# Low halves of the projection weights: two ScalarE copies and an adding DMA in place of a GpSimd subtraction

## The chip, the cores and the metric

One Trainium2 chip, one of its cores. The time is that of one execution on the device in microseconds (us), from runs of the whole kernel; a profile of one execution gives the span from the first to the last instruction and what each engine did in it. Engines are named as in the profile: PE (TensorE matmul), PEld (its weight loads), DVE (VectorE), ACT (ScalarE), POOL (GpSimd), SP (SyncE, which issues most DMAs here).

## What is computed

A hybrid decoder block on 1040 tokens (16 meta tokens and 1024 of the sequence) of width 1024, all in float32:

```python
u = rms_norm(h, norm_mix_g[l])
proj = u @ w_in[l]
q, k, v, r, a_lr, c_in, g_gla, g_conf = jnp.split(proj, pts, axis=-1)
log_a = log_sigmoid(a_lr @ w_alpha_up[l] + b_alpha[l]) / GATE_TAU
o = gla_chunked(qh, kh, vh, ah)            # gated linear attention, 4 heads
br_gla = (rms_norm(o) * silu(r)) @ w_gla_o[l]
c = causal_dwconv(c1 * sigmoid(c2), conf_dw_w[l], conf_dw_b[l])   # 31 taps
br_conf = silu(layer_norm(c)) @ w_conf_o[l]
h = h + (sigmoid(g_gla) * br_gla + sigmoid(g_conf) * br_conf) @ w_out[l]
u = rms_norm(h, norm_ffn_g[l])
a, bv = jnp.split(u @ w_up[l], 2, axis=-1)
h = h + (silu(causal_dwconv(a, ffn_dw_w[l], ffn_dw_b[l])) * bv) @ w_down[l]
```

The change concerns the first product, `u @ w_in`, which with the work laid between its blocks takes the first 875 us.

## The kernel before

**Products in three parts.** Every large product is taken in a rounded type (float32r) and repaired: a number is split into a high half `hi`, the number rounded, and a low half `lo`, the number minus `hi`. `mm3` (lines 169 to 180) issues three matmuls for each piece of 128 input channels: weight `hi` by activation `hi` (L178), weight `hi` by activation `lo` (L179), weight `lo` by activation `hi` (L180). The split of a weight is made on the chip: `load_raw` (L153) has SP load 128 output columns of a weight (512 KB) into one of three buffers `wr`; in `split_w` ACT copies it with rounding into `wh` (L161) and another engine subtracts, `wl = wr - wh` (L162). `wh` and `wl` have three buffers each. Activations are split in the same way by `split` (L218, L219) into `uh` and `ul`.

**The stage.** The projection is 57 blocks: one for the 16 decay channels (`wh_a`, which carries both halves in one tile and has no `wl`), then q, k, v and the two convolution halves c2, c1 of each of four heads, r, and two gates. A block is 72 matmuls: 8 pieces of the input channels, three parts, three chunks of tokens. `next_w` keeps one weight ahead of the block that runs. The weights of blocks 1 to 50 of the list have the subtraction on POOL, those after them on DVE:

```python
wq.append(load_alpha(src) if src is w_alpha else load_w(src, PO if wpos[0] < 51 else V, rate["ahead"]))
```

**What runs between.** Into the blocks the attention steps of a head (`gla`) and the 31-tap convolutions (`conv`) are laid by a rate per evacuated chunk (`tick`). A conv step is one DVE instruction over 128 x 1026 (L361), 240 of them. `gla` alternates between engines: decays on ACT and DVE, exponent tiles E of seven levels, whose left half DVE makes and whose right half POOL makes (L460, L463 and L461, L464), with an exponential on ACT between them (L462), small matmuls on PE, copies of their results into Pt (L485, L502), then the state st from chunk to chunk (L515). kmT (L435) is the transposed key of the meta tokens, which ACT copies out for PE (L437).

**What sets the order.** A scheduler lays the instructions of each engine into one fixed queue ahead of time; each queue runs in order and waits where an operand or a buffer is not ready. Weight loads and splits are given a priority some thousands of instructions ahead of their place (`high_priority`).

Of the kernel before, what the change touches and what calls it, by code (L numbers as in the profile page):

```python
# [11 lines left out]
F32R = mybir.dt.float32r  # L12
U8 = mybir.dt.uint8
AF = mybir.ActivationFunctionType
ALU = mybir.AluOpType

P = 128
# [47 lines left out]
def build(ctx, tc, xT, w_mix, w_o3, w_up, w_dn, w_au, pvec, masks, outT):  # L65
    nc = tc.nc
    V, S, PO, PE = nc.vector, nc.scalar, nc.gpsimd, nc.tensor
# [4 lines left out]
    wspl = ctx.enter_context(tc.tile_pool(name="wspl", bufs=3))  # L72
    sm = ctx.enter_context(tc.tile_pool(name="sm", bufs=2))
    uid = [0]
# [13 lines left out]
    def slot(dt=F32, nm="s"):  # L88
        uid[0] += 1
        return slots.tile([P, SLOT], dt, tag="slot", name=f"{nm}_{uid[0]}")  # L90
# [55 lines left out]
    def pin(ins):  # L146
        if rate["pinned"]:
            tc.keep_in_program_order(ins)

    def load_raw(src):  # L150
        uid[0] += 1
        raw = wraw.tile([P, 1024], F32, tag="raw", name=f"wr_{uid[0]}")[:, : src.shape[-1]]
        nc.sync.dma_start(raw, src)  # L153
        return raw

    def split_w(raw, eng=None):
        uid[0] += 1
        n = raw.shape[-1]
        hi = wspl.tile([P, 1024], F32R, tag="hi", name=f"wh_{uid[0]}")[:, :n]
        lo = wspl.tile([P, 1024], F32R, tag="lo", name=f"wl_{uid[0]}")[:, :n]  # L160
        pin(S.activation(hi, raw, AF.Copy))  # L161
        (eng or V).tensor_tensor(lo, raw, hi.bitcast(F32), op=ALU.subtract)  # L162
        return hi, lo

    def load_w(src, eng=None, ahead=4000):
        with tc.high_priority(offset=ahead):
            return split_w(load_raw(src), eng)

    def mm3(out, whi, wlo, pairs, cols, first=True, last=True):
        n = len(pairs)  # L170
# [126 lines left out]
    def prefetch(n):  # L297
        while wpos[0] < len(seq) and len(wq) < n:
            src = seq[wpos[0]]
            wq.append(load_alpha(src) if src is w_alpha else load_w(src, PO if wpos[0] < 51 else V, rate["ahead"]))  # L300
            wpos[0] += 1
# [511 lines left out]
    def unit_tail(f, a, b, y):  # L813
# [7 lines left out]
        return y  # L821

    heads = [unit_head(load_w(w_up[0]))]
    for _ in due:
        pass
    heads += [unit_head(load_w(w_up[f])) for f in range(1, HEADS_UP)]
    w = slice(0, 2 * HT)
    ws = [unit_weights(0)]
# [62 lines left out]
    for j in range(FT // 2):  # L891
        if j == FT // 2 - 1:
            hi, lo = slot(F32R, "oph"), slot(F32R, "opl")
# [116 lines left out]
```

## Time and profile before

| what | value |
|---|---|
| runs, median (three) | 1897.48 us (1896.18 to 1898.14) |
| profiled execution, span from first to last instruction | 1894.4 us |
| mean granted TensorE clock | 0.980 |
| PE busy | 1786.0 us, 94% |
| DVE busy | 1228.9 us, 65% |
| ACT busy | 669.3 us, 35% |
| POOL busy | 570.3 us, 30% |
| DMA | 174.72 MB, mean 92 GB/s |

The profiled execution is given by its span alone; what lies around it, launch and end, is not in the profile, and the median of the runs is 3.1 us longer than the span. The share of busy time is a mean over stages: the projection ends at about 875 us, the three output products at 1152, the upward product of the feed-forward part at 1620, and the rest is the downward product. Which engine sets the pace of a stretch is read from the views by stretch, and what it waits for from the view of waits; the timeline shows single instructions. A row of the timeline has start, duration, engine, line, operation, and in brackets the idle time of that engine before it with what ended it.

### The profile page before, as it was taken

The page shows a single profiled execution, that of the slowest core. Times are in us where ns is not written, and L with a number is a line of the kernel's source. Part 1 is how long each engine was busy: PE and PEld are TensorE (multiplying, and loading weights), DVE is VectorE, ACT ScalarE, POOL GpSimd, SP SyncE. Part 2 cuts the span into 40 slices and gives each one's busy share as a digit, 9 for nine tenths or more (in the row PEclk, how much of TensorE's full clock was granted, in tenths as well). Part 3 has the DMA queues.
Part 4 walks back from the last instruction along what each step waited for, and adds up shares of the span by engine and source line. Part 5 has one row for each costly group of instructions (what it writes and reads, how often), then busy time and mean ns, then how long its engine had stood idle before and what let it go on. Part 6 is the DMA issues. An engine that isn't in the chain of part 4 may idle for free.

```text
span 1894.4 us, 28989 instructions
## 1 busy us (share of the span) xinstructions
PE 1786.0 (94%) x12210; PEld 1697.8 (90%) x12210; DVE 1228.9 (65%) x1462; ACT 669.3 (35%) x1008; POOL 570.3 (30%) x333
## 2 busy tenths in 40 slices
PE   5998999999899989999999998899999999899997
PEld 3997989898898989999999998899999999677886
DVE  7258969969899494354255467886676676643533
ACT  5314325324333752476132343222222222432321
POOL 3323624624542452210000144533333334200000
PEclk9998999999999999999999999899999999999999
DMA  4111111111110322436122532222212223644541
GB/s 172 45 45 45 35 45 68 34 45 56 45 45 23 101 68 78 156 114 232 51 92 82 195 121 97 68 79 90 79 67 90 79 69 112 248 123 133 165 133 64
DMA packets 56242, 174.72 MB, mean 92 GB/s; under 512 B 6064, under 2 KB 13360, under 8 KB 56112
## 3 DMA queue, kind: packets, MB, share of 16 engines
q1 hardware_dynamic: 51168, 159.03, 25.2%
q0 software_dynamic: 3168, 11.54, 1.7%
q10 hardware_dynamic: 1776, 2.30, 0.4%
q8 instruction: 96, 1.57, 0.4%
q14 instruction: 34, 0.28, 0.0%
HBM read 136.10 MB, written 36.74 MB: 91 GB/s over the span
## 4 chain that ended last, share of the span: by engine, by line
PE 55%; DVE 4%; issue 1%; ACT 0%; POOL 0%; DVEq 0%; ACTq 0%
PE prod L178 12%; PE prod L180 12%; PE prod L179 12%; PE mm L178 6%; PE mm L179 6%; PE mm L180 6%; DVE opl L219 1%; DVE un L713 1%; DVE wl L162 1%; PE g L934 1%; DVE un L831 0%; POOL opl L219 0%; DVE t L228 0%; ACT wh L161 0%; DVE fy L814 0%
## 5 line engine op out<-in xcount | busy, mean ns | idle before, releaser
L178 PE MATMUL mm<-uh,wh 128*128 128x342 f32 (+4 forms) x1344 | 447.8, 333 | 0.0
L179 PE MATMUL mm<-ul,wh 128*128 128x342 f32 (+4 forms) x1344 | 437.9, 326 | 0.0
L180 PE MATMUL mm<-uh,wl 128*128 128x342 f32 (+4 forms) x1344 | 436.2, 325 | 0.0
L361 DVE SCALAR_TENSOR_TENSOR y<-c,pv,y 128x1026 f32<-128x1026 f32 x240 | 390.0, 1625 | 5.2
L161 ACT ACTIVATE wh<-wr 128x1024 fp32r<-128x1024 f32 (+2 forms) x202 | 200.4, 994 | 488.6 <-PE mm L179 182.7
L179 PE MATMUL prod<-opl,wh 128*128 128x258 f32 x1232 | 349.6, 284 | 12.1 <-DVE opl L219 11.6
L178 PE MATMUL prod<-oph,wh 128*128 128x258 f32 x1232 | 349.9, 284 | 4.6 <-DVE t L796 3.5
L180 PE MATMUL prod<-oph,wl 128*128 128x258 f32 x1232 | 350.7, 285 | 0.0
L162 POOL TENSOR_TENSOR wl<-wr,wh 128x1024 fp32r<-128x1024 f32 x68 | 184.8, 2718 | 313.3 <-ACT wh L161 313.3
L162 DVE TENSOR_TENSOR wl<-wr,wh 128x1024 fp32r<-128x1024 f32 (+2 forms) x134 | 156.8, 1172 | 176.0 <-ACT wh L161 170.0
L178 PEld LDWEIGHTS mm<-uh,wh 128*128 128x128 f32 x1344 | 258.1, 192 | 3.9 <-issue 2.1
L179 PEld LDWEIGHTS mm<-ul,wh 128*128 128x128 f32 x1344 | 258.0, 192 | 3.2 <-issue 2.1
L180 PEld LDWEIGHTS mm<-uh,wl 128*128 128x128 f32 x1344 | 258.3, 192 | 0.9 <-issue 0.6
L179 PEld LDWEIGHTS prod<-opl,wh 128*128 128x128 f32 x1232 | 235.0, 191 | 13.2 <-DVE opl L219 12.5
L178 PEld LDWEIGHTS prod<-oph,wh 128*128 128x128 f32 x1232 | 235.1, 191 | 5.6 <-issue 3.2
L180 PEld LDWEIGHTS prod<-oph,wl 128*128 128x128 f32 x1232 | 234.8, 191 | 0.0
L180 PE MATMUL mm<-oph,wl 128*128 128x512 f32 (+1 forms) x374 | 143.8, 385 | 3.2 <-DVE wl L162 3.2
L178 PE MATMUL mm<-oph,wh 128*128 128x512 f32 (+1 forms) x374 | 143.8, 384 | 2.1 <-ACT wh L161 1.3
L179 PE MATMUL mm<-opl,wh 128*128 128x512 f32 (+1 forms) x374 | 144.8, 387 | 0.6 <-DVE opl L219 0.6
L178 PE MATMUL prod<-sh,wh 128*128 128x342 f32 (+2 forms) x448 | 133.6, 298 | 0.5 <-ACT gate L620 0.5
L180 PE MATMUL prod<-sh,wl 128*128 128x342 f32 (+2 forms) x448 | 133.3, 298 | 0.0
L179 PE MATMUL prod<-sl,wh 128*128 128x342 f32 (+2 forms) x448 | 133.3, 297 | 0.0
(238 smaller groups left out, 2763.6 us busy)
## 6 DMA issues: line engine op xcount, KB each, us to landing
wr<-in_w_mix SPq DMA_DIRECT2D x56, 512.0 KB, 3.3
wr<-in_w_up SPq DMA_DIRECT2D x48, 512.0 KB, 3.3
wr<-in_w_o SPq DMA_DIRECT2D x32, 512.0 KB, 3.5
wr<-in_w_dn SPq DMA_DIRECT2D x32, 512.0 KB, 3.6
act_d<-fy SPq DMA_DIRECT2D x21, 512.0 KB, 2.6
ar<-act_d POOLq DMA_DIRECT2D x21, 512.0 KB, 7.1
wr<-in_w_dn SPq DMA_DIRECT2D x16, 384.0 KB, 3.2
y_d<-y SPq DMA_DIRECT2D x8, 513.0 KB, 4.3
```

Of the source, the lines that this page charges most:

```text
L161: pin(S.activation(hi, raw, AF.Copy))
L162: (eng or V).tensor_tensor(lo, raw, hi.bitcast(F32), op=ALU.subtract)
L178: PE.matmul(out, whi[:, wk], hi[:, c0:c1], start=first and k == 0, stop=False)
L179: PE.matmul(out, whi[:, wk], lo[:, c0:c1], start=False, stop=False)
L180: PE.matmul(out, wlo[:, wk], hi[:, c0:c1], start=False, stop=last and k == n - 1)
L219: (eng or V).tensor_tensor(lo, src, hi.bitcast(F32), op=ALU.subtract)
L361: V.scalar_tensor_tensor(y[:, :LQ], c[:, j : j + LQ], pcol("dw_w", i * CONV_K + j), y[:, :LQ], op0=ALU.mult, op1=ALU.add)
L713: V.scalar_tensor_tensor(pair_cols(un[hf][j], 0, width)[:, e], pair_cols(hh[j], 0, width)[:, e], pcol("ffn_g", 2 * j + e), rs[:, :width], ...
L934: PE.matmul(stats[c], ones, sq, start=n == 1, stop=n == KT - 1)
```

## The change

For the 50 weights whose subtraction was on POOL, ACT writes two tiles from the raw weight: the rounded weight with its sign turned into `wl`, and the rounded weight into `wh`. Then POOL issues a DMA that reads the raw weight from memory once more and adds it into `wl`, so that `wl` is raw minus rounded. The other weights (the decay block, the last six of the projection, and all of the later stages) are split as before.

```diff
     def load_w(src, eng=None, ahead=4000):
         with tc.high_priority(offset=ahead):
-            return split_w(load_raw(src), eng)
+            raw = load_raw(src)
+            if eng is not PO:
+                return split_w(raw, eng)
+            uid[0] += 1
+            hi = wspl.tile([P, 1024], F32R, tag="hi", name=f"wh_{uid[0]}")
+            lo = wspl.tile([P, 1024], F32R, tag="lo", name=f"wl_{uid[0]}")
+            pin(S.activation(lo, raw, AF.Copy, scale=-1.0))
+            pin(S.activation(hi, raw, AF.Copy))
+            nc.gpsimd.dma_start(lo, src, accum_op=ALU.add)
+            return hi, lo
```

Nine lines are added, so that what stood at line 173 or below stands nine lines further down: L178 is now L187, L218 is L227. The two copies are L173 and L174, the adding DMA is L175.

The queues change in three places. First ACT at the start of the kernel, from the last steps of the first norm on. Before (`wh` and `wl` are weights, `uh` the activation's high half, x and t512 the input and its squares):

```order
L225 ACTIVATE t512_38_174<-t512_38_174 128x256
L161 ACTIVATE wh_67_363<-wr_66_361 128x1024
L161 ACTIVATE wh_69_369<-wr_68_367 128x1024
L218 ACTIVATE uh_11_106<-x_3_98 128x256
L218 ACTIVATE uh_13_108<-x_4_99 128x256
L218 ACTIVATE uh_15_110<-x_5_100 128x256
L267 ACTIVATE t512_40_206<-x_3_98 128x392
```

The same place of ACT's queue now:

```order
L234 ACTIVATE t512_38_174<-t512_38_174 128x256
L173 ACTIVATE wl_67_364<-wr_66_361 128x1024
L174 ACTIVATE wh_67_363<-wr_66_361 128x1024
L173 ACTIVATE wl_69_371<-wr_68_368 128x1024
L174 ACTIVATE wh_69_370<-wr_68_368 128x1024
L173 ACTIVATE wl_71_378<-wr_70_375 128x1024
L227 ACTIVATE uh_11_106<-x_3_98 128x256
L276 ACTIVATE t512_40_206<-x_3_98 128x392
```

Five weight copies stand ahead of the first activation copy where two stood; the fifth is the low half of the third weight, whose high half comes much later. Second, POOL's queue at that place, with the three adds ahead of the activation's low halves (before, two subtractions stood there):

```order
L175 DMA wl_67_364<-in_w_mix 128x1024
L175 DMA wl_69_371<-in_w_mix 128x1024
L175 DMA wl_71_378<-in_w_mix 128x1024
L228 TENSOR_TENSOR ul_14_109<-x_4_99,uh_13_108 128x256
L228 TENSOR_TENSOR ul_18_113<-x_6_101,uh_17_112 128x256
```

Later in POOL's queue each add stands, but for a few, where the subtraction stood. Third, PE where the first head's kmT is used, in the first v block of the second head (g are the attention's small products, mm the block). Before:

```order
L180 MATMUL mm_164_1415<-uh_15_110,wl_144_1275 128x348
L437 MATMUL g_157_1394<-vmeta_137_1219,kmT_156_1392 128x256
L448 MATMUL g_161_1401<-ident_81,kd_149_1341 128x128 x4
L178 MATMUL mm_164_1415<-uh_17_112,wh_144_1274 128x348
L179 MATMUL mm_164_1415<-ul_18_113,wh_144_1274 128x348
```

Now:

```order
L189 MATMUL mm_164_1427<-uh_15_110,wl_144_1285 128x348
L187 MATMUL mm_164_1427<-uh_17_112,wh_144_1284 128x348
L188 MATMUL mm_164_1427<-ul_18_113,wh_144_1284 128x348
L189 MATMUL mm_164_1427<-uh_17_112,wl_144_1285 128x348
L187 MATMUL mm_164_1427<-uh_19_114,wh_144_1284 128x348
L188 MATMUL mm_164_1427<-ul_20_115,wh_144_1284 128x348
L189 MATMUL mm_164_1427<-uh_19_114,wl_144_1285 128x348
L446 MATMUL g_157_1405<-vmeta_137_1229,kmT_156_1403 128x256
L457 MATMUL g_161_1412<-ident_81,kd_149_1352 128x128 x4
```

The two small products stand six matmuls of the block later; the same holds for the second and third heads.

## Rows read from the trace of the kernel before

**Rows 1.** Stretches: us, busy PE, PEld, DVE, ACT, POOL (instructions), clock, DMA share, GB/s.
```profile
0.00:16.00 16.00, 4.68 (x9) 2.15 (x9) 8.83 (x26) 7.04 (x11) 5.08 (x9) 1.00 0.79 254
50.00:150.00 100.00, 100.00 (x620) 99.91 (x619) 45.43 (x42) 29.89 (x47) 27.64 (x15) 1.00 0.14 48
150.00:200.00 50.00, 41.37 (x286) 39.59 (x285) 45.30 (x48) 16.28 (x29) 22.35 (x11) 0.90 0.15 43
200.00:250.00 50.00, 44.42 (x344) 43.48 (x343) 48.55 (x67) 17.45 (x24) 25.83 (x11) 0.97 0.13 43
```

**Rows 2.** Waits of PE, 60 to 800 us: total, times, longest.
```profile
PE g L437 <- ACT kmT L435: 13.2, 3, 8.6
PE g L476 <- POOL E L464: 11.4, 4, 3.4
PE g L510 <- DVE st L515: 6.6, 5, 2.0
PE g L511 <- DVE Pt L502: 4.9, 3, 2.2
```

**Rows 3.** Timeline, 163 to 174 us, around PE's longest wait.
```profile
163.63 1.29 DVE L361 SCALAR_TENSOR_TENSOR y<-c,pv,y 128x1026 f32<-128x1026 f32 x1
164.84 1.22 DVE L413 TENSOR_TENSOR kd<-kd,k 128x1024 f32<-128x1024 f32 x1
164.87 3.39 POOL L162 TENSOR_TENSOR wl<-wr,wh 128x1024 fp32r<-128x1024 f32 x1 [10.10 <-ACT wh L161]
165.98 3.36 DVE L417 TENSOR_TENSOR qd<-qd,q 128x1024 f32<-128x1024 f32 x1
168.22 4.00 POOL L461 TENSOR_TENSOR E<-nb 128x512 f32<-128x512 f32 x2
169.26 4.05 DVE L361 SCALAR_TENSOR_TENSOR y<-c,pv,y 128x1026 f32<-128x1026 f32 x2
...
173.72 1.22 PE L437 MATMUL g<-vmeta,kmT 16*128 16x256 f32 x2 [8.63 <-ACT kmT L435]
```

**Rows 4.** POOL's groups by line, 150 to 800 us: count, busy us, mean ns.
```profile
L162 POOL TENSOR_TENSOR wl<-wr,wh 128x1024 fp32r<-128x1024 f32 x39 | 113.9, 2921 | 157.5 <-ACT wh L161 157.5
L464 POOL TENSOR_TENSOR E<-E,q 128x512 f32<-128x512 f32 x24 | 52.5, 2197 | 74.3 <-ACT E L462 74.3
L461 POOL TENSOR_TENSOR E<-nb 128x512 f32<-128x512 f32 x24 | 43.2, 1811 | 0.0
```

**Rows 5.** Timeline, 80 to 93 us: ACT's weight copies in the running stretch.
```profile
80.70 1.06 ACT L161 ACTIVATE wh<-wr 128x1024 fp32r<-128x1024 f32 x1 [3.27 <-PE mm L179]
...
92.17 1.06 ACT L161 ACTIVATE wh<-wr 128x1024 fp32r<-128x1024 f32 x1 [3.27 <-PE mm L179]
```

**Rows 6.** Timeline of POOL, 1601 to 1607 us: DMAs that it issues later.
```profile
1606.45 0.72 POOL L862 DMA_DIRECT2D ar<-act_d  x1 [0.18 <-issue]
```

**Rows 7.** DVE's groups by line, 150 to 800 us: the conv steps.
```profile
L361 DVE SCALAR_TENSOR_TENSOR y<-c,pv,y 128x1026 f32<-128x1026 f32 x220 | 358.5, 1630 | 4.6
```

**Rows 8.** DMA issues by line: count, KB each, median us to landing.
```profile
wr<-in_w_mix SPq DMA_DIRECT2D x56, 512.0 KB, 3.3
...
ar<-act_d POOLq DMA_DIRECT2D x21, 512.0 KB, 7.1
```

**Rows 9.** Timeline of the start, 10 to 27 us.
```profile
11.39 1.99 ACT L161 ACTIVATE wh<-wr 128x1024 fp32r<-128x1024 f32 x2
...
12.51 5.04 POOL L162 TENSOR_TENSOR wl<-wr,wh 128x1024 fp32r<-128x1024 f32 x2 [10.34 <-ACT wh L161]
12.89 4.94 DVE L278 SCALAR_TENSOR_TENSOR x<-x,pv,t 128x256 f32<-128x256 f32 x2
15.38 0.42 ACT L218 ACTIVATE uh<-x 128x256 fp32r<-128x256 f32 x1 [2.00 <-DVE x L278]
...
19.55 0.58 PE L175 MATMUL mm<-ul,wh_a 128*128 128x256 f32 x1 [2.91 <-DVE ul L219]
...
26.01 0.28 PE L180 MATMUL mm<-uh,wl 128*128 128x242 f32 x1
```

## Prediction

> **What bounds the kernel now.** I first read the stretches by engine [rows 1]. From 50 to 150 us PE is busy the whole time: there the projection runs at PE's own pace, and nothing that another engine does can shorten it. From 150 us the attention step of a head is interleaved, and PE stands still 8.6 us of the next 50 and 5.6 us of the 50 after, while DVE is busy 45.3 and 48.6 us of 50. So inside a kernel that PE bounds there are places where DVE's queue sets the end. The second view, PE's waits from 60 to 800 us [rows 2], says what those waits end with: the four longest kinds shown sum to 36.1 us (all nine to 50.7), and every one ends at DVE, at POOL's half of the exponent tile E, or at a small ACT copy (kmT). None ends at a weight. Weights are ready long before their use; what the change can give lies in those waits, not in the weights.
>
> Third, the timeline around the longest wait [rows 3]. POOL's weight subtraction starts at 164.87 and takes 3.39 us. DVE's multiplication L413 just before it takes 1.22 us; the next of the same shape, L417, takes 3.36. The two conv steps that follow, beside POOL's L461, take 4.05 us, where one without a neighbour takes 1.29. DVE's queue then reaches the little copy after which ACT writes kmT, and PE has waited 8.63 us. So POOL's two-input arithmetic and DVE's two-input arithmetic hold each other up, and a weight subtraction costs DVE 3.36 - 1.22 = 2.14 us where they meet.
>
> **What the change does, part by part.** All 50 POOL subtractions go; 39 of them lie in the attention's stretch, from 150 to 800 us, and take 113.9 us, 2.92 us each [rows 4]. In place of each, ACT makes a second copy of the raw weight (1.06 us, the price of the present copy [rows 5]), POOL issues a DMA, and the DMA adds the raw weight from memory.
>
> *POOL and DVE.* A DMA that POOL issues now occupies its queue 0.72 us [rows 6], so POOL gets back about 39 x (2.92 - 0.72) = 86 us there. For DVE I take bounds. Above: every subtraction meets a full DVE queue, 39 x 2.14 = 83 us. Below: the 220 conv steps of this stretch take 1630 ns on average [rows 7] against 1.29 us alone [rows 3], 75 us over; the subtractions are 54% of the three POOL groups shown (113.9 of 209.6 us [rows 4]) and about 41% with POOL's other groups, hence 31 us. So DVE gets back 31 to 83 us, mostly in the stretches where it is the one that is late.
>
> *What reaches PE.* PE can get back no more than it waits: 51 us. How much of a wait goes, I take from the longest one. L417 falls back to 1.22 (2.14 us); L461 starts some 2.7 us earlier (3.39 - 0.72), and the two conv steps lose most of their collision (4.05 - 2.58 = 1.5 us); PE now comes to this matmul six weight matmuls later, about 0.16 us each (72 of them in 11.47 us [rows 5]), 0.95 us. Together 4.6 of 8.63, about half. Half of 51 gives **-25 us**; bounds 0 and -51. What is late next is the chain of small steps itself: ACT's exponential, its table loads, PE's own transposes.
>
> *The clock.* It was granted at 0.90 and 0.97 in the two stretches with long waits, and at 1.00 where PE never waited [rows 1]; this falls from 2.4 to 1.2 GHz for a part of the stretch. That is 5.0 + 1.5 = 6.5 us of full speed lost beside 14.2 us of standing, partly while PE stood anyway. At the same ratio 25 us of waits carry up to 11 us; I take **-4**, bounds 0 and -11.
>
> *ACT.* 39 more copies in this stretch are 41 us on an engine that is busy 16 to 17 us of 50 here [rows 1]. Nothing is gained or lost where it idles, but ACT works in order, and a copy that stands before an exponential or before kmT delays that chain by 1.06 us. One such place for each of four heads: **+4**; bounds 0 and +12.
>
> *The new latency, in the running stretch.* The copy of a weight starts when a buffer of three comes free, and the next one starts 11.47 us later [rows 5]; the weight is used two blocks on, 22.9 us after its copy began. After two copies (2.1 us) and the issue (0.7 us) 20 us remain for the add to land. A load of the same 512 KB that POOL issues lands in 7.1 us, a plain SP load in 3.3 [rows 8]. What the addition costs on top no row shows; the 20 us cover it up to 2.8 times the slower row. I take 0.
>
> *The start.* ACT now makes five weight copies, not two, before the first activation copy. They start at 11.39, 1.0 us each, so that copy moves from 15.38 to 16.4, +1.0. DVE in turn is free: its first two normalisations take 4.94 us beside two subtractions [rows 9], against some 0.43 for the other two-input steps of that width there; PE's wait of 2.91 us for DVE's first low half [rows 9] mostly goes. The transfers are the risk: in the first 16 us the core already moves 254 GB/s [rows 1], and the three adds of that place bring 1.5 MB, 6 us at this rate, in between the loads of x. The first low half is needed at 26.0 [rows 9]; ACT is done with it at 12.4, the issue ends at 13.2, plus 7.1 is 20.3. I take **+1**, bounds -3 and +7.
>
> What the trace cannot price is the addition itself. The Trainium skill, "Collectives: The Full Stack", in "The bandwidth ceiling: the fold count and why AG ≠ RS ≠ AR", says that an addition in the DMA reads two sources for each write and so moves at half the rate of a copy. No run here shows it yet; as an estimate from that page the 7.1 us would become at most 14.2, the first add would land at 27.4, 1.4 us after its use, and the sum would be -22.6 instead of -24.
>
> **The sum.** -25 - 4 + 4 + 1 = -24 us on the profiled span of 1894.4, hence 1870.4. The runs that were timed have a median of 1897.48, 3.1 above that span; the forecast in their terms is **1873.5 us**.
>
> **The rivals.** *The waits stay.* If PE's waits come from the steps' own latencies and not from DVE's load, the freed time only becomes idle time on DVE and POOL, and ACT's second copy takes back the rest: 1897 us, within 0.2% (3.8 us, about what a measurement of this kernel tells from no change). For it: many of the waits are under 2.5 us and recur alike in every head. Against it: DVE is 97% busy from 200 to 250 us. A variant is that the change does not free the port at all, because the issue of an adding DMA occupies POOL as long as the subtraction; the 0.72 us row speaks against it. Chance 0.14.
>
> *Nearly all of the waits go.* Then -45 with the clock, -5 to -8 more: 1848. DVE's gain (31 to 83 us) is enough for it; fixed latencies speak against it. Chance 0.09.
>
> *The add comes late (slower).* If an add takes more than 20 us to land, or the queue passes fewer than one in 11.47 us, each block in the PE-bound stretches waits for its low half. The cycle of buffers then sets the pace: two blocks last as long as copies, issue and add. With 24 us to land that is (24 + 2.8 - 22.9) / 2 = 1.9 us for each of some 25 blocks without attention work between them, 48 us, less half of the gain, plus the start: about 1925. It decides from 20 us on; at 18 us only the start suffers (+6). The nearest rows, 3.3 and 7.1, speak against it, but they are copies, and the type is converted as well. Chance 0.12, and another 0.05 for a start that loses more than the rest gains.
>
> **How the numbers follow.** The forecast's own case has 0.60, with 1860 to 1890 from its bounds. Faster by over 0.2%: 0.60 plus 0.09, plus some of the rival without gain: 0.71. Within 0.2%: 0.12. Slower: 0.17. A range of 1855 to 1902 leaves out the lower half of the large gain and most of the late adds, about 2 in 10.
>
> **What will show it.** Right: no POOL subtraction before 800 us; L361 near 1.4 us on average; L417 near 1.3; PE's waits from 60 to 800 us near 25 us, that for kmT under 5; adds that land in 7 to 15 us; POOL's issue near 0.7. Wrong: PE waiting for wl; an add of 20 us or more; an issue that takes POOL 2 us and DVE steps still at 3.3 beside it; the first 60 us longer by more than 5; or DVE clearly idle in the attention steps while PE waits as long as before.

## The result, and the profile after

The changed kernel takes **1853.66 us** (median of four runs, 1851.55 to 1856.32), beside 1897.28 for the kernel before on the same chip (four runs, 1896.18 to 1898.14): ratio 0.9769, 95% interval 0.9757 to 0.9781, so 43.6 us faster. The direction was forecast, the size was not: 1853.66 lies 1.3 us under the range, near the rival in which nearly all of the waits go (1848). The profiled execution has a span of 1852.3 us, 42.1 less than before. Of the runs below, one of e1, at a granted clock of 0.556, took 2900.43 us, and e1's median leaves it out.

The views are read in the order of the prediction. First the stretches of the kernel after (us, busy PE, PEld, DVE, ACT, POOL with instructions, granted clock, DMA share, GB/s):

```profile
150.00:200.00 50.00, 45.38 (x327) 43.56 (x325) 48.82 (x54) 28.40 (x41) 15.63 (x13) 1.00 0.36 78
200.00:250.00 50.00, 50.00 (x379) 49.66 (x380) 38.67 (x63) 19.00 (x27) 14.50 (x11) 0.97 0.36 85
60.00:800.00 740.00, 721.35 (x4911) 698.83 (x4910) 521.48 (x663) 352.93 (x562) 197.67 (x143) 1.00 0.41 97
```

And the last of these stretches in the kernel before:

```profile
60.00:800.00 740.00, 688.98 (x4616) 663.09 (x4615) 548.17 (x632) 284.71 (x482) 298.09 (x141) 0.97 0.18 59
```

Against [rows 1], PE stands still 4.6 us from 150 to 200 instead of 8.6, and not at all from 200 to 250, where DVE has become idle for 11 of 50 us. Over 60 to 800 us PE is idle 18.7 us instead of 51.0, and the mean granted clock is 1.00 instead of 0.97. ACT works 68 us more there, at no visible cost; POOL 100 us less.

PE's waits of the kernel after, 60 to 800 us (total, times, longest), answer to [rows 2]:

```profile
PE g L485 <- POOL E L473: 10.0, 4, 4.6
PE g L550 <- DVE t L544: 4.6, 4, 1.7
PE g L507 <- DVE E L472: 2.6, 2, 1.7
PE g L435 <- DVE km L433: 1.4, 1, 1.4
```

These are all of them, 18.6 us where 50.7 stood. The waits for kmT (13.2), st (6.6) and Pt (4.9) are gone. What is left is POOL's own half of E, almost as long as before (10.0 us, 11.4 there), and short steps that recur in each head.

The groups after, 150 to 800 us (count, busy us, mean ns, idle before), DVE and then POOL, answer to [rows 7] and [rows 4]:

```profile
L370 DVE SCALAR_TENSOR_TENSOR y<-c,pv,y 128x1026 f32<-128x1026 f32 x222 | 318.5, 1435 | 4.8 <-DVE pms L438 0.3
```

```profile
L473 POOL TENSOR_TENSOR E<-E,q 128x512 f32<-128x512 f32 x24 | 54.0, 2262 | 80.2 <-ACT E L471 80.2
...
L175 POOL DMA_DIRECT2D wl<-in_w_mix x39 | 34.1, 875 | 215.6 <-ACT wl L173 215.4 <-issue 0.2
```

A conv step takes 1435 ns on average, 195 less than the 1630 before, which over 222 of them is 43 us; the issue of an add occupies POOL 0.88 us. The DMA issues after (count, KB each, median us to landing), against [rows 8]:

```profile
wr<-in_w_mix SPq DMA_DIRECT2D x56, 512.0 KB, 3.9
wl<-in_w_mix POOLq DMA_DIRECT2D x50, 512.0 KB, 7.8
...
ar<-act_d POOLq DMA_DIRECT2D x21, 512.0 KB, 6.9
```

All 50 adds together, from the view of line L175:

```profile
DMA to landing us min/median/max: 5.2/7.8/10.6
```

The slowest add lands in 10.6 us, half of the 20 that are there. PE never waits for a low half.

**Where the longest wait went.** DVE and POOL of the kernel before, from its timeline at 139 to 174 us, earlier than [rows 3] begin, with the PE instruction that stands at the beginning of the block:

```profile
139.17 2.98 POOL L162 TENSOR_TENSOR wl<-wr,wh 128x1024 fp32r<-128x1024 f32 x1 [8.90 <-ACT wh L161]
140.25 12.26 DVE L361 SCALAR_TENSOR_TENSOR y<-c,pv,y 128x1026 f32<-128x1026 f32 x8
151.90 2.87 POOL L162 TENSOR_TENSOR wl<-wr,wh 128x1024 fp32r<-128x1024 f32 x1 [9.75 <-ACT wh L161]
152.42 4.93 DVE L350 TENSOR_TENSOR_SCAN nb<-r,l 128x16 f32<-128x16 f32 x9
...
163.40 0.28 PE L427 MATMUL g<-ident,km 128*16 128x128 f32 x1
...
173.23 0.14 DVE L430 COPY pms<-g 15x1 f32<-15x1 f32 x1
```

The same instructions in the kernel after, and the two multiplications of [rows 3] (L422 and L426 now):

```profile
144.05 10.55 DVE L370 SCALAR_TENSOR_TENSOR y<-c,pv,y 128x1026 f32<-128x1026 f32 x8
155.13 2.72 DVE L359 TENSOR_TENSOR_SCAN nb<-r,l 128x16 f32<-128x16 f32 x9 [0.53 <-ACT l L357]
...
165.73 1.22 DVE L422 TENSOR_TENSOR kd<-kd,k 128x1024 f32<-128x1024 f32 x1
166.87 1.22 DVE L426 TENSOR_TENSOR qd<-qd,q 128x1024 f32<-128x1024 f32 x1
168.00 2.60 DVE L370 SCALAR_TENSOR_TENSOR y<-c,pv,y 128x1026 f32<-128x1026 f32 x2
168.37 0.28 PE L436 MATMUL g<-ident,km 128*16 128x128 f32 x1
170.52 0.14 DVE L439 COPY pms<-g 15x1 f32<-15x1 f32 x1
170.69 0.27 ACT L444 ACTIVATE kmT<-g 16x128 f32<-16x128 f32 x1
171.01 0.69 PE L446 MATMUL g<-vmeta,kmT 16*128 16x256 f32 x2
```

The copy pms stands in DVE's queue just after PE's products of the block. Measured from the PE instruction of the same place it comes after 9.83 us before (173.23 - 163.40) and after 2.15 now (170.52 - 168.37): DVE reaches it 7.68 us sooner. With the 0.95 us by which PE's use stands later that is 8.63 us, which is the wait that PE had: kmT is now ready at 170.96 and PE takes it at 171.01, just in time and no more.

Where the 7.68 us arise is read off the same way. At the multiplication L413 (164.84, now 165.73) DVE is already 4.08 us sooner; the other 3.60 are the collisions of [rows 3] behind it. Of the earlier part, 1.71 us come from the eight conv steps at 140 (12.26, now 10.55) and 2.21 from the nine scans at 152 (4.93, now 2.72): two **earlier** subtractions had held DVE up, one and two blocks ahead, and its queue had no idle time since in which to lose that delay. DVE also comes to the eight conv steps 1.17 us sooner (from where is not traced), and it gives about 1 us back where it now waits itself, as the 0.53 us before the scans. The other waits were not followed back row by row.

**Where the rest went.** The first matmul of the third block after the decay block begins at 69.1 us before and 74.1 after; the last gate's block (the 56th) at 863.1 and 819.6. So the start lost 5.0, and from there the heads gained 48.5. Of these, PE's waits are 32.1 (50.7 - 18.6). In the records of the granted clock the lower level, 1.2 GHz, holds for 37.5 us between 60 and 760 us before and for 3.4 after. In 5.3 of the 37.5 PE stood, nearly all of it in the longest wait. The stretch around it in the kernel before (columns as in [rows 1]), and two of PE's matmuls behind the wait, three steps apart:

```profile
168.50:178.70 10.20, 4.97 (x17) 4.33 (x18) 8.73 (x9) 0.86 (x2) 4.76 (x3) 0.50 0.34 90
```

```profile
176.65 0.49 PE L178 MATMUL mm<-uh,wh 128*128 128x348 f32 x1
177.53 0.49 PE L178 MATMUL mm<-uh,wh 128*128 128x348 f32 x1
```

Three matmuls take 0.88 us there, 0.29 each, against 0.16 at the upper level (72 in 11.47 us [rows 5]), so a us of work at the lower level loses 0.45. That gives (37.5 - 5.3 - 3.4) x 0.45 = 13.0 us. Together 45.1; the remaining 3.4 of the 48.5 are not accounted for.

### The profile page after: what moved, and what is told of

It reads as the page before. It is cut to its first block, busy times and chain, and to the rows that moved or that the text cites. A ratio compares the mean times of both kernels' runs of the same rounds, so it can differ in the third digit from the quotient of the medians.

```text
span 1852.3 us, 29073 instructions
## 1 busy us (share of the span) xinstructions
PE 1772.4 (96%) x12210; PEld 1688.0 (91%) x12210; DVE 1164.0 (63%) x1462; ACT 707.8 (38%) x1052; POOL 458.2 (25%) x333
## 4 chain that ended last, share of the span: by engine, by line
PE 54%; DVE 5%; DMA 1%; issue 1%; ACT 1%; POOL 0%; DVEq 0%; ACTq 0%
PE prod L187 12%; PE prod L189 12%; PE prod L188 12%; PE mm L188 6%; PE mm L187 6%; PE mm L189 6%; DVE opl L228 1%; DVE wl L162 1%; DVE un L722 1%; DMA ar<-act_d 1%; PE g L943 1%; DMA wr<-in_w_dn 1%; DVE un L840 0%; DVE fy L825 0%; POOL opl L228 0%
## 5 line engine op out<-in xcount | busy, mean ns | idle before, releaser
L187 PE MATMUL mm<-uh,wh 128*128 128x342 f32 (+4 forms) x1344 | 444.8, 331 | 0.0
L187 PE MATMUL prod<-oph,wh 128*128 128x258 f32 x1232 | 350.5, 285 | 4.6 <-DVE t L805 3.5
L370 DVE SCALAR_TENSOR_TENSOR y<-c,pv,y 128x1026 f32<-128x1026 f32 x240 | 341.7, 1424 | 5.4 <-DVE pms L438 0.3
L161 ACT ACTIVATE wh<-wr 128x1024 fp32r<-128x1024 f32 (+2 forms) x152 | 147.8, 975 | 382.3 <-PE prod L188 175.3
L187 PEld LDWEIGHTS mm<-uh,wh 128*128 128x128 f32 x1344 | 255.0, 190 | 4.1 <-issue 2.1
L187 PEld LDWEIGHTS prod<-oph,wh 128*128 128x128 f32 x1232 | 235.0, 191 | 5.7 <-issue 3.2
L187 PE MATMUL mm<-oph,wh 128*128 128x512 f32 (+1 forms) x374 | 143.5, 384 | 2.1 <-ACT wh L161 1.3
L187 PE MATMUL prod<-sh,wh 128*128 128x342 f32 (+2 forms) x448 | 133.8, 299 | 0.5 <-ACT gate L629 0.5
L175 POOL DMA_DIRECT2D wl<-in_w_mix x50 | 43.8, 877 | 306.7 <-ACT wl L173 306.5
```

The costliest lines, as they stand in the source:

```text
L175: nc.gpsimd.dma_start(lo, src, accum_op=ALU.add)
L187: PE.matmul(out, whi[:, wk], hi[:, c0:c1], start=first and k == 0, stop=False)
L370: V.scalar_tensor_tensor(y[:, :LQ], c[:, j : j + LQ], pcol("dw_w", i * CONV_K + j), y[:, :LQ], op0=ALU.mult, op1=ALU.add)
```

## Experiments

Each kernel ran beside the kernel before on the same chip; the kernel before took 1897.28 to 1898.48 us (medians) in the four series, so a difference between two changed kernels is uncertain by some 1 us. The order is that of the questions.

**Is it POOL's reading of two operands?** e1 puts the subtraction back as an additional instruction that reads and writes as before (into the raw weight, whose value then no one uses), and keeps all else of the change:

```diff
             nc.gpsimd.dma_start(lo, src, accum_op=ALU.add)
+            PO.tensor_tensor(raw, raw, hi.bitcast(F32), op=ALU.subtract)
             return hi, lo
```

> The changed kernel, but POOL also makes the old subtraction after each adding DMA, into the raw buffer, where nobody reads it. Theory A (POOL's subtraction and DVE's two-input steps hold each other up, and DVE's lateness is what PE waits for): the gain is gone, 1893 to 1908 us (the old time plus the 5 us that the start lost), conv steps back at about 1.6 us. Theory B (POOL's queue is what counts, its halves of E come late behind the subtraction): the same, 1893 to 1908. Theory C (the scheduler's new order of PE and DVE gives the gain): still 1850 to 1862.

Measured: 1914.97 us (median of three runs), ratio 1.0088 (1.0073 to 1.0103). The whole gain is gone, and it is 17 us slower than the kernel before, above the 1908 us that both theories allowed. One more run gives its profile:

> The kernel of the changed kernel plus a POOL subtraction into the raw weight after each adding DMA, once more, for its profile. Interference: conv steps at 1.6 us or more on average from 150 to 800 us, and PE's waits from 60 to 800 us at 45 to 60 us, as before the change; span about 1912. If the subtraction acted through POOL's queue alone: conv steps near 1.42 us.

Measured: 1917.58 us in one run, span 1915.8. DVE's and POOL's groups, 150 to 800 us, and PE's waits, 60 to 800 us:

```profile
L371 DVE SCALAR_TENSOR_TENSOR y<-c,pv,y 128x1026 f32<-128x1026 f32 x224 | 376.7, 1682 | 4.8
```

```profile
L176 POOL TENSOR_TENSOR wr<-wr,wh 128x1024 f32<-128x1024 f32 x39 | 106.2, 2722 | 0.0
```

```profile
PE g L486 <- POOL E L474: 18.9, 4, 7.0
PE g L447 <- ACT kmT L445: 11.6, 3, 8.4
PE g L520 <- DVE st L525: 7.1, 4, 2.5
```

The kmT and st waits are back with nearly their old size; all waits are 62.5 us, a little over what was expected, with the largest rise at POOL's half of E (18.9 us, 11.4 before), in whose queue the subtraction now stands beside the adds' issues. The time at 1.2 GHz is 54.6 us. Theory C, the new order, goes too: in this run the first head's products with kmT stand as late among PE's matmuls as in the changed kernel (fifteen of the block behind the transpose, nine before the change), and PE waits 8.4 us for kmT all the same.

e2 takes the place of the subtraction with work that occupies POOL about as long and reads nothing:

```diff
             nc.gpsimd.dma_start(lo, src, accum_op=ALU.add)
+            for _ in range(3):
+                PO.memset(raw, 0.0)
             return hi, lo
```

> The changed kernel, and POOL writes zeros three times over the raw buffer after each adding DMA: POOL is as long busy as with the subtraction (3 x 0.95 = 2.9 us) and the buffer is freed as late, but POOL reads nothing. Theory A (what hurts is POOL reading two operands beside DVE): 1853 to 1864 us, conv steps at about 1.4 us. Theory B (POOL's queue time): 1880 to 1900, with POOL's E as the longest wait of PE. Theory C (order): 1850 to 1862.

Measured: 1858.67 us, ratio 0.9792 (0.9778 to 0.9805). POOL's group, 150 to 800 us, DVE's group there, and PE's longest kind of wait:

```profile
L177 POOL MEMSET wr<- 128x1024 f32 x118 | 126.2, 1069 | 3.0
```

```profile
L372 DVE SCALAR_TENSOR_TENSOR y<-c,pv,y 128x1026 f32<-128x1026 f32 x223 | 316.7, 1420 | 4.9 <-DVE pms L440 0.3
```

```profile
PE g L487 <- POOL E L475: 11.4, 4, 4.1
```

POOL spends 126 us on the memsets, more than the 113.9 of the subtractions [rows 4], and the conv steps stay at 1420 ns; kmT and st do not come back. POOL's time in its own queue is worth some 5 us at most (1858.67 - 1853.66, and the intervals of the two ratios just touch); the 56 us from here to e1 are its two-operand arithmetic beside DVE's. The Trainium skill, "SBUF — State Buffer", in "Who interferes with whom", says that a VectorE instruction with two inputs from SBUF contends with a GpSimd instruction that reads SBUF, and not with one that only writes it: the 1420 ns beside memsets and the 1682 beside subtractions agree.

**Is it DVE's load?** e3 is the kernel before with all splits on DVE: the interference goes, but DVE gets the subtractions.

```diff
-load_w(src, PO if wpos[0] < 51 else V, rate["ahead"])
+load_w(src, V, rate["ahead"])
```

> The kernel before with all subtractions on DVE: no adding DMA, no second ACT copy, POOL as free as it can be. Theory A with DVE's load as the limit: DVE is spared 2.1 us for each collision and pays 1.2 us for the subtraction, so a bit under half of the gain: 1870 to 1885. Theory B (POOL's queue): the full gain without the loss at the start, 1845 to 1856. Theory C (order): near 1897 unless the order happens to move likewise.

Measured: 1859.81 us, ratio 0.9798 (0.9784 to 0.9811), between the two expectations. DVE's groups, 150 to 800 us:

```profile
L361 DVE SCALAR_TENSOR_TENSOR y<-c,pv,y 128x1026 f32<-128x1026 f32 x220 | 312.8, 1422 | 4.0
L162 DVE TENSOR_TENSOR wl<-wr,wh 128x1024 fp32r<-128x1024 f32 x44 | 57.3, 1303 | 44.6 <-ACT wh L161 44.6
```

A subtraction takes 1.30 us on DVE and 2.92 on POOL. PE's waits fall to 24.7 us, and from the third block to the 56th the kernel gains 33.6 of the 48.5 us. The engines over that same work, in the kernel before and in e3 (columns as in [rows 1]):

```profile
69.14:863.10 793.96, 742.93 (x4956) 715.87 (x4955) 582.21 (x661) 332.81 (x532) 301.37 (x141) 0.98 0.20 66
```

```profile
65.60:826.00 760.40, 735.23 (x4956) 709.78 (x4956) 569.81 (x707) 331.76 (x530) 173.94 (x93) 0.99 0.21 69
```

DVE's total falls by only 12.4 us (582.2 to 569.8) where the kernel gains 33.6, and its share of the stretch rises (73% to 75%). So its total does not account for the gain; that it was held up at places where PE needed it next does fit, as the longest wait shows, but no run tests the places by themselves. With no adding DMA at all, 38.7 of the 43.6 us were to be had (1898.48 - 1859.81); its third block begins at 65.6, 3.5 us ahead of the kernel before.

**Does the gain come step by step, or at a threshold?** e9 gives every second weight from the fifth on back to POOL:

```diff
-            if eng is not PO:
+            if eng is not PO or (wpos[0] > 4 and wpos[0] % 2):
                 return split_w(raw, eng)
```

> The changed kernel, with every second weight from the fifth on split by POOL's subtraction again (23 of 50; some 19 of the 39 of the attention's stretch). Theory proportional (each subtraction costs where it meets DVE, whatever the others do): half of the 48.5 us that the heads gained, so about 1853.7 + 24 = 1878 (1870 to 1885), with conv steps near 1.53 us and PE's waits from 60 to 800 us near 35. Rival threshold (the waits go as soon as DVE and POOL have enough slack): 1855 to 1864, PE's waits under 25.

Measured: 1872.48 us, ratio 0.9865 (0.9849 to 0.9882), conv steps 1534 ns. PE's waits, 60 to 800 us, the ones that came back:

```profile
PE g L446 <- ACT kmT L444: 3.9, 1, 3.9
PE g L519 <- DVE st L524: 3.9, 3, 1.4
```

All waits are 28.8 us, and 20.5 us at 1.2 GHz. The heads gain 29.5 of 48.5 us, with 19 of 39 subtractions left in their stretch. It is nearer the proportional theory (1878, 1870 to 1885) than the threshold, though the first half of them brought more (29.5) than the second (19.0).

**What does the second ACT copy cost?** e8 writes the high half twice, which doubles the suspected cost:

```diff
             pin(S.activation(hi, raw, AF.Copy))
+            pin(S.activation(hi, raw, AF.Copy))
```

> The changed kernel with a third ACT copy for each of the 50 weights (the high half is written twice), 1.06 us each: doubles the cost that the forecast put at +4 us (0 to +12). Theory free (ACT idles where the copies fall): 1852 to 1857, of which up to 3 us are the start, where three more copies stand. Theory priced (a copy delays the chain to an exponential or to kmT): 1858 or more, with PE's waits from 60 to 800 us up by 4 us or more.

Measured: 1852.97 us, ratio 0.9762 (0.9748 to 0.9777), waits 17.7 us. ACT is busy 404.6 us from 60 to 800 us instead of 352.9, and neither the time nor PE's waits are longer. The copies are free here, so the second one is too.

**What does the start lose?** First whether it repeats:

> The changed kernel once more, unaltered, to see how far the start repeats. If the lost 5 us of the start are the change's own, block 3 starts at 73.5 to 74.7 again; if they are partly chance of this one execution (two stretches at the low clock there), it starts anywhere from 71 to 75. PE's waits from 60 to 800 us 18 to 20, half-clock time there 3 to 10 us.

Measured: 1854.4 us in one run, third block at 73.9, waits 18.6 us, 10.2 us at 1.2 GHz between 60 and 760. So the late start repeats; the clock's share of the heads varies by some 2 us between these executions: of the 10.2 us PE stood 2.7, which leaves (7.5 - 3.4) x 0.45.

e4 gives only the first three weights back to POOL's subtraction:

```diff
-            if eng is not PO:
+            if eng is not PO or wpos[0] < 4:
                 return split_w(raw, eng)
```

> The changed kernel, but the first three weights are split as before, with POOL's subtraction. If the 5 us that the start lost come from what the change does to the first three weights (adds between the loads of x, five ACT copies ahead of the first activation copy), the first v block starts at 69 instead of 74 us and the time is 1847 to 1851. If the start is later for another reason, 1853 as before. The rest of the gain must stay.

Measured: 1850.68 us, ratio 0.9747 (0.9733 to 0.976), third block at 70.2. Of the 5.0 us 3.9 come back there, and 3.0 in the run (the intervals of the two ratios overlap a little). e6 and e7 separate two causes. e6 has the start of e4 and moves low halves out to a scratch nobody reads, by DMAs that POOL issues (traffic without ACT's copies). e7 keeps ACT's copies and overwrites the negated one by POOL's subtraction (ACT's order without the adds' traffic):

```diff
+            if wpos[0] < 4:
+                hi, lo = split_w(raw, eng)
+                scr = dr.tile([P, 1024], F32, name=f"scr{wpos[0]}")
+                nc.gpsimd.dma_start(scr, lo.bitcast(F32))
+                return hi, lo
```

> The kernel with the first three weights split by POOL's subtraction, and each of their three low halves also stored to a scratch in memory by a DMA that POOL issues: three transfers of 512 KB stand where the adds stood, without ACT's additional copies. Theory traffic (the start loses because the three adds move 1.5 MB among the loads of x): the start is late again, block 3 at 73 to 74, 1852 to 1855. Theory order (it loses because five ACT copies stand ahead of the first activation): block 3 at 70 to 71, 1849 to 1852.

```diff
-            nc.gpsimd.dma_start(lo, src, accum_op=ALU.add)
+            if wpos[0] < 4:
+                PO.tensor_tensor(lo, raw, hi.bitcast(F32), op=ALU.subtract)
+            else:
+                nc.gpsimd.dma_start(lo, src, accum_op=ALU.add)
```

> The changed kernel with ACT's two copies kept for the first three weights, but their low halves then written by POOL's subtraction and not by an adding DMA: the order of ACT without the traffic (the negated copy is overwritten). Theory order: block 3 at 73 to 74, 1852 to 1855. Theory traffic: block 3 at 70 to 72, 1849 to 1852.

Measured: e6 1851.01 us (ratio 0.9735 to 0.9764), third block at 71.7; e7 1850.75 us (0.9735 to 0.9768), third block at 72.3. Neither cause alone costs the run its 3 us: each is as fast as e4 and moves the third block by 1.5 and 2.1 us. Two of e6's three stores fell in the first 60 us, so its traffic was less than that of the adds. Against a simple sum speaks e8, which has adds and copies and began its third block at 71.9.

Two things the traces do show. The loads of x at the start (196 KB) land in 8.3 to 8.6 us (median) in the runs with the three adds there (the changed kernel, e2, e8 to e11) and in 4.2 to 5.2 in those without (the kernel before, e3 to e7; e7, with the copies alone, has 4.3): the adds make them late, not the copies. And the lower clock goes with a later third block: from 20 to 60 us the mean granted clock is 0.91 before. Of the kernels whose first three weights are split as in the changed one, it is 0.87 in e8 and e10 (third block at 71.9 and 72.5), 0.83 in the changed kernel, 0.79 in e9 and e11 (73.7 and 73.9) and 0.70 in e2 (75.2). That the clock is the cause and not a consequence is not shown, and e6 and e7 were later than e4 at its 0.87 or above. How the 5 us divide stays open.

ACT at the start of the changed kernel, timeline, 16 to 29 us, against [rows 9]:

```profile
16.01 1.04 ACT L173 ACTIVATE wl<-wr 128x1024 fp32r<-128x1024 f32 x1
16.95 0.40 ACT L227 ACTIVATE uh<-x 128x256 fp32r<-128x256 f32 x1
...
21.63 0.53 ACT L276 ACTIVATE t<-x 128x392 f32<-128x392 f32 x1 [1.68 <-DMA x<-in_xT]
...
24.72 0.53 ACT L278 ACTIVATE t<-x 128x392 f32<-128x392 f32 x1 [2.25 <-DMA x<-in_xT]
...
27.80 0.53 ACT L276 ACTIVATE t<-x 128x392 f32<-128x392 f32 x1 [2.25 <-DMA x<-in_xT]
```

The first activation copy comes at 16.95 (15.38 before), and then ACT waits three times for the input, 6.2 us; the kernel before has no such wait there. The loads of x that land in 4.2 us (median, 196 KB) before now take 8.4. In e11 the three waits are there again (5.7 us).

**A version that beats both.** e5 splits the first three weights on DVE, which the changed kernel leaves idle for more than half of the time from 15 to 30 us (6.1 of 15 busy):

```diff
-            if eng is not PO:
-                return split_w(raw, eng)
+            if eng is not PO or wpos[0] < 4:
+                return split_w(raw, V)
```

> The changed kernel, with the first three weights split by a VectorE subtraction instead of two ScalarE copies and an adding DMA. Theory A (in the running stretch the change gains by taking POOL's two-input work away, at the start it loses by what it puts there): the start is that of the kernel with all splits on DVE (block 3 at about 65.6 us against 74.1), and the heads are those of the changed kernel: 1844 to 1848. Rival (the order of the start decides when DVE's later work falls, so an earlier start is waited away again in the first head): 1850 to 1854.

Measured: **1847.2 us**, ratio 0.9732 (0.9717 to 0.9746), against 0.9757 to 0.9781 for the change alone; waits 17.7 us. DVE and ACT at its start, timeline, 13 to 15 us:

```profile
13.95 0.48 DVE L287 SCALAR_TENSOR_TENSOR x<-x,pv,t 128x256 f32<-128x256 f32 x1
14.35 1.22 DVE L162 TENSOR_TENSOR wl<-wr,wh 128x1024 fp32r<-128x1024 f32 x1
14.47 0.42 ACT L227 ACTIVATE uh<-x 128x256 fp32r<-128x256 f32 x1 [1.05 <-DVE x L287]
```

Where two normalisations took 4.94 us beside two subtractions on POOL [rows 9], one takes 0.48 here and a whole subtraction 1.22; the first activation copy comes at 14.47, the third block at 66.4. The gain of the start (2.7 us against before) and that of the heads (47.7) add up.

## Why the prediction was too small

**What bounds the kernel: right.** PE's waits in the attention stretch, fed by DVE that POOL's subtractions hold up, were the place. e1, e10 and e2 show the cause; kmT, st and Pt vanish from the list, conv steps fall to 1.42 to 1.44 us as foreseen, the issue of an add is 0.88 us (0.7 foreseen).

**"Half of 51 gives -25 us": this step failed.** It measured 32.1: the waits for kmT, st and Pt went whole. The half came from the longest wait, of which the text counted 4.6 of 8.63 us, by the collisions in the ten microseconds that rows 3 show. The subtractions ahead of them, at 139.17 and 151.90, were left out; DVE stood 4.08 us later by then, and kept that delay because its queue had no idle time up to the copy. Counted with them, the same working gives the whole wait. It is covered with 0.05 us to spare; a little less, and a part of it would have stayed. Those that remain end at POOL's half of E or are short fixed steps; there the argument of fixed latencies, which the prediction set against the rival, does hold, for 18.6 us and not for half.

**"The clock: I take -4": this step failed by more.** It measured -13.0 in this execution and, by the same working, -11.1 in the repeat, both at or beyond the bound of -11. The ratio that the text had worked out was nearly right: 6.5 us lost beside 14.2 of standing, for 32.1 us of waits, is 14.7. The choice was wrong, to count only a third of it because PE partly stood anyway: in the 150 to 250 us that the text read, PE stood 5.2 of the 13.6 us at the lower level, but over all heads only 5.3 of 37.5. Waits and time at 1.2 GHz lie together in the runs: 62.5 and 54.6 us in e10, 50.7 and 37.5 before, 28.8 and 20.5 in e9, 24.7 and 17.1 in e3; the runs with waits of 17.6 to 20.2 us have 3.4 to 13.7. That the waits cause the low clock is how these runs lie; no run changed the clock alone.

**"ACT: +4": not there.** e8 doubles the copies and nothing gets later.

**"The start: +1": +5.0, inside the bounds of -3 and +7.** The first activation copy moved by 1.6 us (+1.0 foreseen) and the waits for x came on top; the text had named the transfers as the risk and chosen the low value. The prediction listed a first 60 us longer by more than 5 as a sign against it: it is at that bound, and the heads cover it ten times. The transfers that it named did come late, by the adds.

**The new latency: right.** No add takes 20 us, none is waited for. By the estimate from the half rate in the Trainium skill, "Collectives: The Full Stack", section "The bandwidth ceiling: the fold count and why AG ≠ RS ≠ AR", an add would have landed in up to 14.2 us; it landed in 7.8, so the trace doesn't show the rule in the landing. What the DMA engines spend comes near it. The queues of the kernel after, 60 to 800 us (packets, MB, share of 16 engines; q0 carries only the adds there):

```profile
q1 hardware_dynamic: 12816, 46.70, 20.8%
q0 software_dynamic: 6768, 24.64, 19.7%
```

That is 0.80% for a MB of adds and 0.45% for one of plain transfers, 1.8 times as much. It is not the price of POOL's queue: the same queue from 1560 to 1850 us, with the loads `ar` and one store of 512 KB and no add:

```profile
q0 software_dynamic: 3168, 11.54, 11.4%
```

That is 2.9 us of all 16 engines for a MB (11.4% of 290 us), against 5.9 for a MB of adds (19.7% of 740 us), 2.1 times. What of it is the addition and what the conversion to float32r, which these loads lack, no run separates.

**The sum**, with what was measured: -32 - 13 + 0 + 5 = -40 us, against a span shorter by 42.1. One price of a rival does not follow from its terms: 48 us for late adds on 1897.5, less half of the 24, plus a start of up to 7, is 1933 to 1941 and not 1925. Nothing else rests on it, and no add came late.

## What to carry to other kernels

Where an engine's queue is full, read a wait back to the last idle time of the engine that is late, not only over the rows next to the wait: every hold-up since then is in it, and removing them all can remove it whole. Then price the lower clock as a part of the same term, since in these runs the time at 1.2 GHz fell with the waits. And take a new mechanism only where it pays: here an adding DMA serves the running stretch, while at the start, with the input still loading, a subtraction on the idle VectorE was 6.5 us better.

## What was not expected of the hardware

Work on POOL that only writes (126 us of memsets) left DVE's two-input steps at 1420 ns, where subtractions of 106 us put them at 1682. And an add of 512 KB that costs the DMA engines 1.8 to 2.1 times a plain transfer still lands within 0.9 us of the plain load that POOL issues (7.8 beside 6.9): its cost shows with others, as the weight's own load, which takes 3.9 instead of 3.3 us, and the loads of x at the start, 8.4 instead of 4.2.
